# A hybrid Hyena and RG-LRU block: side work handed out at the middle and the end of each in-projection block, gates one lane's gate at a time

## The chip, the core and the metric

One core of a Trainium2 chip. The metric is device time of one execution in us. The engines are TensorE (PE in the profile; its weight loads are PEld), VectorE (DVE), ScalarE (ACT), GpSimd (POOL) and SyncE (SP, which here only issues DMAs). Each engine works through its own queue in order.

## What is computed

One layer of a diffusion block over 4096 latent tokens (width 1024) and 256 context tokens. A modulated RMSNorm feeds one in-projection whose 3072 columns are six groups of 512: `x0`, `x1`, `v` and gate `zh` of a long convolution (done as an FFT), `xr` and gate `zr` of a two-directional gated recurrence. In short:

```
p = (rms_norm(x) * (1 + sc) + sh) @ w_in
xc = dwconv(xr); r = sigmoid(xc @ wa + ba); i = sigmoid(xc @ wx + bx)      # per head, per direction
a = exp(-8 * r * softplus(-lam)); b = sqrt(1 - a*a) * (i * xc); h = scan(a, b)
y = concat(rms_norm(long_conv(v * x1) * x0) * silu(zh), rms_norm(h_fwd + h_bwd) * silu(zr))
out = rms_norm(x + g * (y @ w_out))
```

## The kernel before, in words

Values are split into two f16 halves, so a product is three matmuls (hi*hi, hi*lo, lo*hi). Channels lie on the 128 partitions; a group of 512 columns is four blocks `j` (`NB` = 4), and tokens come in eight chunks `i` of 512 (`NB` and `i` make one **in-projection block**: `inproj`, 8 x 3 = 24 matmuls of 128x512 into a PSUM tile `mm`, of which there are three).

**Pass A** (`pass_a`) goes through chunks 0 to 7, 12 blocks each: four of `xr`, then `x1` and `v` alternating. `OX[i]` says how many of the others go ahead of `xr`. After each block come its short convolution (`conv`, ScalarE then VectorE) and stores. Beside the blocks run: the load, normalisation and split of the next chunk's input tile X (`xload` at places `XK`, its squares on ScalarE, L429, at a later step, then `xsplit` with GpSimd's `xlo` and transposing DMAs into X); the forward recurrence of the chunk (`units_a`, two `unit`s of two lanes each); the Hyena filter (`filter_group`: four exponentials into `dec` on ScalarE every `FD` = 4.95 steps; `filter_row`: three matmuls into `fa`, `kd`, `kh`; its `second` part three matmuls into `fb`, an evacuation `vk`, a store to VkD). The context tokens go once through `ctx_in` in chunk 0.

**Pass B** (`blocks_b`) goes through 24 triples (chunk, name) of four blocks each, `zr`, `x0`, `zh` from chunk 7 down, with the backward recurrence (`units_b`), and pulls FFT steps from a generator: `rate` per block, first 64 steps of `s1u_gen` (two matmuls into `fa`, evacuation `vo`), then slots (`slot_gen`: five loads, 24 small matmuls into `fa` and `fb`, an inverse of a slot before, stores), then parts of the inverse. **Phase out** does the last FFT part and the out-projection; the change does not touch it.

**`unit`** is a generator with one stage per `next`: split of `xc` into `xh`; the gates (per lane and gate three matmuls `xh,gh` into `fa` for the gate written to `R` or `fb` for `I`, and a sigmoid, L824, that empties the bank; then `pmul` on GpSimd); tanh, exp and a square; sqrt; the scan (L849, then `car`, L851). Two units run side by side in a `zip`, so one `next` issues a stage of both.

**The order of the work** is set by a step counter: `at(d, f)` files `f` under the step `d` from now, and `tick`, called after each block, runs what is due. `DA` holds the steps of the recurrence after the last `xr` block in chunk 0, chunk 1 and the others, `DC` those of the context, `DS` and `D0` those of pass B. Side matmuls go through `mms`, which files them 64 instructions later in priority than they stand; a planner then orders each engine's queue when the program is built, by priority and by what its own model says is ready. PSUM has eight banks: three `mm`, two `fa`, two `fb` and one `sm`.

Of the kernel before, what the change touches and what calls it, by code (L numbers as in the profile page):

```python
# [42 lines left out]
FL = (2, 3)  # L43
SIDE = 64
FG = 2
OX = (0, 0, 0, 0, 0, 0, 2, 0)
ET = mybir.EngineType
MS = ()
XS = ((1, 2), (1, 2))
# [1 line left out]
FD = 4.95  # L51
XK = ((6, 9), (1, 6))
NX = 11
D0 = (8, 11, 12, 13, 14, 16, 17, 17)
WO = (9, 13, 16)
SEQ = [(2, "zr"), (2, "x0"), (1, "x0"), (1, "zr"), (0, "x0"), (0, "zh"), (0, "zr"), (2, "zh"), (1, "zh")]
XL = [(6, "zr"), (5, "zr"), (4, "zr"), (3, "zr"), (2, "zr"), (1, "x0"), (0, "x0"), (2, "zh")]
DS = (1, 4, 7, 7, 9, 9, 10)
DA = ((11, 12, 14, 15, 15), (3, 4, 4, 6, 6), (0, 3, 5, 6, 8))
EPS = 1e-6  # L60
MAGIC = 1.5 * 2.0 ** 23
INV2PI = 1.0 / (2.0 * math.pi)
# [100 lines left out]
class K:  # L163
# [334 lines left out]
            w[5] = self.tap_scales(pool, name, j, es[:, 0:1], be[:, 0:1])  # L498
        yield w

    def inproj(self, w, xs):
        ps = self.pst("mm", 3)
        c = 0
        for x in xs:
            n = x.shape[-1]
            i = 0
            for k in range(8):
                for (wi, xi) in ((0, 0), (0, 1), (1, 0)):
                    self.mm(ps[:, c:c + n], w[0][:, wi, k, :], x[:, xi, k, :], i == 0, i == 23)
                    i += 1  # L510
            c += n
        return ps
# [48 lines left out]
    def at(self, d, f):  # L561

        self.todo.setdefault(self.step + d, []).append(f)

    def tick(self):
        for f in self.todo.pop(self.step, []):
            f()
        self.step += 1
# [10 lines left out]
    def pass_a(self):  # L579
        tc, nc, a = self.tc, self.nc, self.a  # L580
        with ExitStack() as es, ExitStack() as right:
# [79 lines left out]
            for i in range(8):  # L661
                xcs = []
                for k, nm in enumerate(names[4:4 + OX[i]] + names[:4] + names[4 + OX[i]:]):
                    if i < 7 and k in XK[i > 0]:
                        h = XK[i > 0].index(k)
                        if h == 0:
                            Xn = self.xtile()
                        xr = self.xload(ap, tok(4 * (i + 1) + 2 * h), 4 * (i + 1) + 2 * h, lag=XS[i > 0][0])
                        self.at(XS[i > 0][1], lambda xr=xr, d=dst(Xn, 2 * h): self.xsplit(ap, xr, self.s1, self.sx, d, IA[1]))
                        if h and i < 5:  # L670
                            self.at(XS[i > 0][1] + 1, lambda i=i, X=Xn: nc.sync.dma_start(self.XD[i + 1], X))
                    j = nm[1]
                    ps = self.inproj(W[nm], [X])
                    p0 = 512 * i - 1 + (1 if i == 0 else 0)
                    if nm[0] == "xr":
                        if j % 2 == 0:
                            xcs.append(hy.tile([128, 1028], F32, name="xc", bufs=4))
                        t = xcs[-1]
                        n = 511 + (i > 0) + (i == 7)
                        c0 = n * (j % 2)  # L680
                        halo[nm] = self.conv(hy, f"xr{j}", ps, W[nm][5], 3, i, i == 7, halo[nm], t, c0 - (i == 0))
                        nc.sync.dma_start(self.xcD[j][:, p0:p0 + n], t[:, c0:c0 + n])
                        if j == 3:
                            for t, d in enumerate(DA[min(i, 2)]):
                                if t == 0:
                                    us = []
                                    self.at(d, lambda us=us, p0=p0, n=n, xcs=xcs: us.append(self.units_a(self.rn, p0, n, xcs)))
                                self.at(d, lambda us=us: next(us[0]))
                    else:
                        b = {"x1": 4, "v": 8}[nm[0]]  # L690
                        t = hy.tile([128, 514], F32, name="cv" + nm[0], bufs=2)
                        halo[nm] = self.conv(hy, f"{nm[0]}{j}", ps, W[nm][5], 2, i, i == 7, halo[nm], t, 0)
                        cnt = 512 - (i == 0) + (i == 7)
                        o = t[:, int(i == 0):int(i == 0) + cnt]
                        if b == 4:
                            o1 = o
                        else:
                            nc.vector.tensor_mul(o1, o1, o)
                            nc.sync.dma_start(self.uD[j][:, p0:p0 + cnt], o1)
                            nc.scalar.activation(o, o1, AF.Square, accum_out=self.usq[:, j, i:i + 1])  # L700
                    if i == 7:
                        self.prep(self.WB, nb[k])
                    self.tick()
                if i >= 6:
                    self.X[i] = X
                X = Xn
# [96 lines left out]

    def unit(self, pool, lanes, n, xc, fin, sig=None):

        nc = self.nc
        L = len(lanes)
        x2 = xc[:, :2 * n]
# [7 lines left out]
        for l, (d, j) in enumerate(lanes):  # L816
            for g, dst, bias in ((0, R, 68 + 4 * d + j), (1, I, 76 + 4 * d + j)):
                for q0 in range(0, n, 512):
                    m = min(512, n - q0)
                    c = n * (j % 2) + q0  # L820
                    ps = self.pst("fa" if g == 0 else "fb", 2)
                    for k, (gi, xi) in enumerate(((0, 0), (0, 1), (1, 0))):
                        self.mms(ps[:, :m], self.gh[d][:, gi, j, g, :], xh[:, 1026 * xi + c:1026 * xi + c + m], k == 0, k == 2)
                    nc.scalar.activation(dst[:, n * l + q0:n * l + q0 + m], ps[:, :m], AF.Sigmoid,  # L824
                                         bias=self.ccol(bias), scale=self.rg[d])
        if sig:
            sig()
        for l in range(0, L, 2):
# [123 lines left out]
    def filter_group(self, pool, g):  # L952

        nc = self.nc
        grp = [4 * g + 4 + k for k in range(4)] if g < 15 else [1, 2, 3, 0]
        hb = self.hb[g % 2]
        n0 = min(grp)
        for h in range(2):
            nc.sync.dma_start(hb[64 * h:64 * h + 64, :, :, 64 * h:64 * h + 64],
                              self.hD[64 * h:64 * h + 64, :, n0:n0 + 4, :])  # L960
        dec = pool.tile([128, 4, 512], F32, name="dec", bufs=1)
        for k, n in enumerate(grp):
            nc.scalar.activation(dec[:, k], self.dl, AF.Exp, scale=self.dcol[:, n:n + 1])
        for k, n in enumerate(grp):
            self.at(1 + k, lambda k=k, n=n: self.filter_row(pool, n, hb[:, :, n - n0, :], dec[:, k]))

    def filter_row(self, pool, n, hb, dec):
        nc = self.nc
        if len(self.sec) > 1:
            self.sec.pop(0)()  # L970
        ps = self.pst("fa", 2)
        for x, (hi, wi) in enumerate(((0, 0), (0, 1), (1, 0))):
            self.mms(ps, hb[:, hi, :], self.whl[:, wi, :], x == 0, x == 2)
# [50 lines left out]
    def blocks_b(self, hy, rn):  # L1024
# [9 lines left out]
        for q, (i, nm) in enumerate(seq):  # L1034
# [14 lines left out]
                    self.at(d, lambda g=st[i]: next(g))  # L1049
            for j in range(NB):  # L1050
                w = W[nm, j]
                ps = self.inproj(w, [X[i]])
                if nm == "zr":
                    if j % 2 == 0:
                        z = rn.tile([128, 1024], F32, name="zr", bufs=2)
# [10 lines left out]
                    if i in (5, 4):  # L1066
                        self.pull(gate, 1)
                self.tick()
                done += rate
                while done >= 1:  # L1070
                    done -= 1
                    self.pull(fft, 1)
# [19 lines left out]
    def units_b(self, rn, i):  # L1092
# [14 lines left out]
        def sig(p):  # L1107
            def f():
# [4 lines left out]
        us = zip(*[self.unit(rn, [(1, 2 * p), (1, 2 * p + 1)], 512, xcs[p],  # L1113
                             lambda h, p=p: self.padd(hfs[p], hfs[p], h[:, :1024]), sig(p) if i else None)
                   for p in range(2)])
        for _ in range(4):
            next(us)
            yield
        next(us)
# [431 lines left out]
```

## Time and profile before

| what | value |
|---|---|
| median of 3 runs | 2286.21 us (2283.73 to 2293.96) |
| the profiled execution | 2286.44 us |
| its span, first to last instruction | 2284.6 us |
| mean granted TensorE clock | 0.927 of 2.4 GHz |
| busy: PE, DVE, ACT, POOL | 84%, 66%, 50%, 38% |

The page and the views of the trace are read in this form: an arrow `out<-in` names tiles; a wait "PE fa L168 <- ACT R L824: total, times, longest" is idle time of PE before an instruction that works on `fa`, ended by the ScalarE instruction of line 824 that writes or reads `R`. L168 is the helper through which all matmuls go, so they are told apart by tiles. Times in timelines and windows are us from the start of the span. Windows name busy time in the order PE, PEld, DVE, ACT, POOL. A matmul's own length is longer than its share of TensorE, since matmuls overlap. Pass A's chunk 3 begins at 421.3, chunk 4 at 521.7, chunk 5 at 618.7 and chunk 6 at 723.6.

### The profile page before, as it was taken

To read this page: it belongs to the slowest core of one execution; us is meant where nothing else is said; L and a number is where in the kernel's file an instruction comes from. 1 tells how busy PE (TensorE), PEld (TensorE's weight loads), DVE (VectorE), ACT (ScalarE), POOL (GpSimd) and SP (SyncE) were. 2 spreads that over 40 slices of the span, in tenths; PEclk is the share of its full clock that TensorE was granted. 3 is DMA by queue.
4 is the path that set the end of the run, shared out by engine and by line. 5 is a ranking of instruction groups with operands and counts; after the bars stand their busy time and mean duration, and the time that the engine had idled before them with its cause. 6 is when DMAs were issued, how large, how long until landed. Compare 5 with 4: busy or idle time off the path is not lost. (4 is left out here: it accounts for less than half of the span.)

```text
span 2284.6 us, 30912 instructions
## 1 busy us (share of the span) xinstructions
PE 1920.0 (84%) x10858; PEld 919.7 (40%) x10858; DVE 1498.6 (66%) x2871; ACT 1151.6 (50%) x1803; POOL 862.5 (38%) x571
## 2 busy tenths in 40 slices
PE   6967769989797889878888999797897766999987
PEld 2434324334343334433334555454544433444433
DVE  4895876857576677664644664755756645777776
ACT  3655766665646577575563633645444412422222
POOL 3024655554656453131322443534433321333330
PEclk9988979989898999999899999998998887999999
DMA  9546244435453322566646999899997799454531
GB/s 291 172 115 168 77 137 137 154 81 162 138 150 96 112 87 96 179 196 207 208 143 210 205 217 249 200 227 244 221 257 206 189 270 230 136 163 155 168 120 74
DMA packets 397608, 391.13 MB, mean 171 GB/s; under 512 B 209513, under 2 KB 295935, under 8 KB 392846
## 3 DMA queue, kind: packets, MB, share of 16 engines
q1 hardware_dynamic: 376988, 342.25, 54.2%
q10 hardware_dynamic: 20466, 46.93, 7.2%
q8 instruction: 85, 1.39, 0.3%
q14 instruction: 69, 0.57, 0.1%
HBM read 213.96 MB, written 132.13 MB: 151 GB/s over the span
## 5 line engine op out<-in xcount | busy, mean ns | idle before, releaser
L168 PE MATMUL mm<-X,wh 128*128 128x512 f16 x3072 | 745.8, 389 | 35.4 <-DMA X<-xh 7.5
L168 PEld LDWEIGHTS <-wh 128*128 128x128 f16 x3648 | 326.5, 100 | 466.9 <-issue 102.3
L168 PE MATMUL mm<-X,wz 128*128 128x512 f16 x1536 | 384.8, 395 | 7.5 <-ACT zh L1064 4.5
L168 PEld LDWEIGHTS <-wz 128*128 128x128 f16 x1728 | 159.9, 101 | 226.7 <-issue 58.0
L168 PEld LDWEIGHTS <-hl 128*128 128x128 f16 x1536 | 151.8, 101 | 212.2 <-issue 20.8
L168 PE MATMUL mm<-wz,hl 128*128 128x512 f16 x768 | 181.8, 395 | 18.9 <-DVE hl L1465 13.4
L168 PE MATMUL mm<-X,hl 128*128 128x512 f16 x768 | 179.9, 389 | 7.7 <-DVE wh L1479 5.3
L985 POOL TENSOR_TENSOR kh<-kd,kh 128x512 f16<-128x512 f32 x64 | 84.5, 1321 | 157.4 <-ACT kh L984 157.4
L460 POOL TENSOR_TENSOR I<-I,xc 128x1024 f32<-128x1024 f32 (+3 forms) x36 | 84.1, 2340 | 128.8 <-ACT I L824 114.8
L1241 POOL TENSOR_TENSOR A<-A,B 128x256 f32<-128x256 f32 x64 | 51.0, 797 | 205.9 <-DVE B L1240 187.8
L452 POOL TENSOR_TENSOR xlo<-xt,xh 128x1024 f16<-128x1024 f32 x32 | 76.8, 2414 | 135.8 <-ACT xh L450 135.8
L168 PE MATMUL fb<-tb,vki 128*128 128x128 f16 x768 | 98.1, 225 | 20.6 <-DMA tb<-in_t_s 19.7
L168 PE MATMUL fa<-xh,gh 128*128 128x512 f16 (+3 forms) x228 | 67.4, 396 | 52.2 <-ACT R L824 42.8
L460 POOL TENSOR_TENSOR zr<-zr,sg 128x1024 f32<-128x1024 f32 x16 | 39.1, 2443 | 176.1 <-ACT sg L1110 176.1
L460 POOL TENSOR_TENSOR xh<-R 128x1024 f32<-128x1024 f32 (+2 forms) x34 | 69.4, 2044 | 79.2 <-ACT R L835 77.7
L1252 DVE SCALAR_TENSOR_TENSOR yy<-A,yy 128x512 f16<-128x512 f32 x64 | 57.7, 902 | 62.1 <-ACT yy L1251 62.0
L841 DVE SCALAR_TENSOR_TENSOR xc<-xh,xc 128x1024 f32<-128x1024 f32 (+2 forms) x34 | 58.2, 1714 | 60.7 <-POOL xh L460 60.3
L168 PE MATMUL fa<-tb,vu 128*128 128x128 f16 x768 | 97.0, 225 | 0.0
L457 POOL TENSOR_TENSOR acc<-acc,dec 128x512 f32<-128x512 f32 x64 | 93.7, 1464 | 4.9 <-ACT dec L978 4.9
L849 DVE TENSOR_TENSOR_SCAN I<-R,car,I 128x512 f32<-128x512 f32 (+2 forms) x64 | 94.6, 1502 | 0.1
L168 PEld LDWEIGHTS <-gh 128*128 128x128 f16 x456 | 46.7, 105 | 111.6 <-issue 70.5
L168 PEld LDWEIGHTS <-vki 128*128 128x128 f16 x768 | 76.7, 100 | 33.7 <-issue 24.5
(377 smaller groups left out, 3723.4 us busy)
## 6 DMA issues: line engine op xcount, KB each, us to landing
VkD<-vk SPq DMA_DIRECT2D x64, 256.0 KB, 2.0
VuD<-vo SPq DMA_DIRECT2D x64, 256.0 KB, 2.5
X<-XD SPq DMA_DIRECT2D x8, 2048.0 KB
vu<-VuD SPq DMA_DIRECT2D x128, 128.0 KB, 3.3
vki<-VkD SPq DMA_DIRECT2D x128, 128.0 KB, 3.6
ZD<-zo SPq DMA_DIRECT2D x64, 256.0 KB, 4.3
xt<-in_x SPq DMA_DIRECT2D x30, 512.0 KB, 5.1
XD<-X SPq DMA_DIRECT2D x6, 2048.0 KB
```

Source lines behind the costliest of these rows:

```text
L168: self.nc.tensor.matmul(out, lhsT, rhs, start=start, stop=stop)
L452: nc.gpsimd.tensor_sub(xl, xt, xh)
L457: self.nc.gpsimd.tensor_add(out, x, y)
L460: self.nc.gpsimd.tensor_mul(out, x, y)
L841: nc.vector.scalar_tensor_tensor(Z, M, 1.0, Z, op0=OP.add, op1=OP.mult)
L849: nc.vector.tensor_tensor_scan(f(h), f(r), f(h), 0.0 if c is None else c, op0=OP.mult, op1=OP.add)
L985: nc.gpsimd.tensor_sub(kh[:, 1], kd, kh[:, 0])
L1241: nc.gpsimd.tensor_sub(A[:, :, 0, :], A[:, :, 0, :], B[:, :, 1, :])
L1252: nc.vector.scalar_tensor_tensor(yy[:, :, 1, :], yv, 0.125, yy[:, :, 0, :], op0=OP.mult, op1=OP.subtract)
```

## The change

Each in-projection block gets a second place for side work, ahead of the fifth of its eight k steps: `inproj` calls `mid` there, which runs what `at` has filed under a half step (and `tick` runs it if no block did). In `unit` the gate stage is split: a `yield` after each lane's gate but the last, so 4 stages take the place of 1 for two lanes, 8 for the context's four. The tables `DC`, `DA`, `DS` and `D0` are longer to match and name half steps. In chunk 1 four other blocks go ahead of `xr`. A filter row's `second` goes to the middle of the block whose end runs the next row. In pass B the FFT generator is pulled at both places, with half the rate each.

```
--- before.py
+++ after.py
@@ -26,7 +26,7 @@
 FFT = 1.75
 INV = 1.65
 LAG = 3
-DC = (1, 2, 4, 5, 5)
+DC = (1, 2, 2, 2.5, 2.5, 3, 3, 3.5, 3.5, 4, 5, 5)
 CT = 5
 ML = 1
 MK = 1
@@ -43,7 +43,7 @@
 FL = (2, 3)
 SIDE = 64
 FG = 2
-OX = (0, 0, 0, 0, 0, 0, 2, 0)
+OX = (0, 4, 0, 0, 0, 0, 2, 0)
 ET = mybir.EngineType
 MS = ()
 XS = ((1, 2), (1, 2))
@@ -51,12 +51,12 @@
 FD = 4.95
 XK = ((6, 9), (1, 6))
 NX = 11
-D0 = (8, 11, 12, 13, 14, 16, 17, 17)
+D0 = (8, 11, 11.5, 12, 12.5, 13, 13, 14, 16, 17, 17)
 WO = (9, 13, 16)
 SEQ = [(2, "zr"), (2, "x0"), (1, "x0"), (1, "zr"), (0, "x0"), (0, "zh"), (0, "zr"), (2, "zh"), (1, "zh")]
 XL = [(6, "zr"), (5, "zr"), (4, "zr"), (3, "zr"), (2, "zr"), (1, "x0"), (0, "x0"), (2, "zh")]
-DS = (1, 4, 7, 7, 9, 9, 10)
-DA = ((11, 12, 14, 15, 15), (3, 4, 4, 6, 6), (0, 3, 5, 6, 8))
+DS = (1, 3, 3.5, 4.5, 5.5, 7, 7, 9, 9, 10)
+DA = ((11, 12, 12.5, 13, 13.5, 14, 15, 15), (1, 2, 2.5, 3, 3.5, 4, 5, 6), (0, 2, 2.5, 3.5, 4.5, 6, 7, 9))
 EPS = 1e-6
 MAGIC = 1.5 * 2.0 ** 23
 INV2PI = 1.0 / (2.0 * math.pi)
@@ -498,13 +498,15 @@
             w[5] = self.tap_scales(pool, name, j, es[:, 0:1], be[:, 0:1])
         yield w
 
-    def inproj(self, w, xs):
+    def inproj(self, w, xs, mid=None):
         ps = self.pst("mm", 3)
         c = 0
         for x in xs:
             n = x.shape[-1]
             i = 0
             for k in range(8):
+                if mid and k == 4:
+                    mid()
                 for (wi, xi) in ((0, 0), (0, 1), (1, 0)):
                     self.mm(ps[:, c:c + n], w[0][:, wi, k, :], x[:, xi, k, :], i == 0, i == 23)
                     i += 1
@@ -562,7 +564,12 @@
 
         self.todo.setdefault(self.step + d, []).append(f)
 
+    def mid(self):
+        for f in self.todo.pop(self.step - 0.5, []):
+            f()
+
     def tick(self):
+        self.mid()
         for f in self.todo.pop(self.step, []):
             f()
         self.step += 1
@@ -670,7 +677,7 @@
                         if h and i < 5:
                             self.at(XS[i > 0][1] + 1, lambda i=i, X=Xn: nc.sync.dma_start(self.XD[i + 1], X))
                     j = nm[1]
-                    ps = self.inproj(W[nm], [X])
+                    ps = self.inproj(W[nm], [X], self.mid)
                     p0 = 512 * i - 1 + (1 if i == 0 else 0)
                     if nm[0] == "xr":
                         if j % 2 == 0:
@@ -803,6 +810,7 @@
 
     def unit(self, pool, lanes, n, xc, fin, sig=None):
 
+
         nc = self.nc
         L = len(lanes)
         x2 = xc[:, :2 * n]
@@ -823,6 +831,8 @@
                         self.mms(ps[:, :m], self.gh[d][:, gi, j, g, :], xh[:, 1026 * xi + c:1026 * xi + c + m], k == 0, k == 2)
                     nc.scalar.activation(dst[:, n * l + q0:n * l + q0 + m], ps[:, :m], AF.Sigmoid,
                                          bias=self.ccol(bias), scale=self.rg[d])
+                if (l, g) != (L - 1, 1):
+                    yield
         if sig:
             sig()
         for l in range(0, L, 2):
@@ -962,12 +972,11 @@
         for k, n in enumerate(grp):
             nc.scalar.activation(dec[:, k], self.dl, AF.Exp, scale=self.dcol[:, n:n + 1])
         for k, n in enumerate(grp):
+            self.at(0.5 + k, lambda: len(self.sec) > 1 and self.sec.pop(0)())
             self.at(1 + k, lambda k=k, n=n: self.filter_row(pool, n, hb[:, :, n - n0, :], dec[:, k]))
 
     def filter_row(self, pool, n, hb, dec):
         nc = self.nc
-        if len(self.sec) > 1:
-            self.sec.pop(0)()
         ps = self.pst("fa", 2)
         for x, (hi, wi) in enumerate(((0, 0), (0, 1), (1, 0))):
             self.mms(ps, hb[:, hi, :], self.whl[:, wi, :], x == 0, x == 2)
@@ -1049,7 +1058,15 @@
                     self.at(d, lambda g=st[i]: next(g))
             for j in range(NB):
                 w = W[nm, j]
-                ps = self.inproj(w, [X[i]])
+
+                def mid():
+                    nonlocal done
+                    self.mid()
+                    done += rate / 2
+                    while done >= 1:
+                        done -= 1
+                        self.pull(fft, 1)
+                ps = self.inproj(w, [X[i]], mid)
                 if nm == "zr":
                     if j % 2 == 0:
                         z = rn.tile([128, 1024], F32, name="zr", bufs=2)
@@ -1066,7 +1083,7 @@
                     if i in (5, 4):
                         self.pull(gate, 1)
                 self.tick()
-                done += rate
+                done += rate / 2
                 while done >= 1:
                     done -= 1
                     self.pull(fft, 1)
@@ -1113,7 +1130,7 @@
         us = zip(*[self.unit(rn, [(1, 2 * p), (1, 2 * p + 1)], 512, xcs[p],
                              lambda h, p=p: self.padd(hfs[p], hfs[p], h[:, :1024]), sig(p) if i else None)
                    for p in range(2)])
-        for _ in range(4):
+        for _ in range(7):
             next(us)
             yield
         next(us)
```

## Rows read from the trace of the kernel before

**Rows 1.** The page, its parts 1 (busy time of each engine) and 2 (40 slices)
```profile
PE 1920.0 (84%) x10858; PEld 919.7 (40%) x10858; DVE 1498.6 (66%) x2871; ACT 1151.6 (50%) x1803; POOL 862.5 (38%) x571
...
PEclk9988979989898999999899999998998887999999
```
**Rows 2.** Windows view: stretch and length, engines' busy time (instructions), clock, DMA share, GB/s
```profile
206.00:917.00 711.00, 604.83 (x2803) 264.24 (x2804) 494.09 (x865) 459.07 (x771) 376.18 (x235) 0.92 0.41 121
917.00:1854.00 937.00, 795.35 (x5112) 408.36 (x5110) 551.69 (x867) 471.24 (x683) 315.08 (x221) 0.94 0.81 212
```
**Rows 3.** Waits view of PE from 206 to 917: total, times, longest
```profile
PE fa L168 <- ACT R L824: 32.7, 6, 14.5
PE fb L168 <- DVE car L851: 14.0, 1, 14.0
...
PE fb L168 <- DVE vk L996: 11.0, 2, 10.4
PE mm L168 <- DMA X<-xh: 7.5, 2, 4.9
PE mm L168 <- DMA X<-xlo: 6.5, 4, 2.8
```
**Rows 4.** Windows view of stretches of pass A, five of them with gates
```profile
421.30:473.90 52.60, 51.88 (x228) 22.58 (x229) 47.93 (x77) 27.25 (x51) 28.02 (x20) 0.95 0.53 171
473.90:501.00 27.10, 15.80 (x61) 6.44 (x60) 5.59 (x13) 17.87 (x30) 12.87 (x9) 0.75 0.36 104
501.00:521.70 20.70, 18.32 (x86) 8.16 (x84) 19.96 (x26) 15.52 (x23) 18.20 (x10) 1.00 0.27 63
...
575.80:600.70 24.90, 17.20 (x62) 6.73 (x61) 6.79 (x15) 16.58 (x29) 15.38 (x11) 0.73 0.41 129
...
674.00:702.80 28.80, 14.33 (x56) 5.85 (x55) 5.31 (x11) 16.36 (x29) 14.27 (x11) 0.70 0.40 105
...
780.90:816.50 35.60, 28.30 (x116) 11.94 (x115) 18.87 (x37) 22.30 (x38) 22.36 (x16) 0.90 0.38 106
816.50:821.60 5.10, 5.10 (x25) 2.30 (x24) 1.63 (x3) 5.09 (x9) 1.62 (x1) 1.00 0.40 76
270.70:306.00 35.30, 21.22 (x85) 8.70 (x84) 23.63 (x32) 26.70 (x42) 16.49 (x11) 0.76 0.22 74
```
**Rows 5.** Timeline of PE from 477 to 492: start, length in us, what
```profile
478.02 0.38 PE L168 MATMUL mm<-X,wz 128*128 128x512 f16 x1
489.71 0.59 PE L168 MATMUL fa<-xh,gh 128*128 128x512 f16 x1 [11.30 <-ACT R L824]
```
**Rows 6.** Timeline of ACT from 477 to 492
```profile
484.92 0.60 ACTq L414 DMA_DIRECT2D rp<-in_t_pos  x1
485.57 0.30 ACT L536 ACTIVATE hax<-cvx,sg 128x2 f32<-128x2 f32 x1 [5.21 <-POOL xt L457]
...
487.58 1.28 ACT L824 ACT_TABLE_LOAD   x1
488.88 0.78 ACT L824 ACTIVATE R<-fa,col,p2r_g 128x512 f32<-128x512 f32 x1
```
**Rows 7.** Waits view of PE from 180 to 207 (context gates)
```profile
PE fa L168 <- ACT R L824: 7.2, 2, 6.3
```
**Rows 8.** Windows and waits (PE) of pass B
```profile
1245.00:1700.00 455.00, 402.54 (x2938) 226.90 (x2937) 279.24 (x442) 217.90 (x351) 180.81 (x163) 0.97 0.94 224
...
PE fa L168 <- DVE vo L1201: 32.3, 13, 8.9
PE fb L168 <- DMA tb<-in_t_s: 19.7, 13, 3.4
...
PE fa L168 <- ACT R L824: 3.3, 2, 2.1
```
**Rows 9.** Groups by form, ACT, 206 to 917: table loads
```profile
L963 ACT ACT_TABLE_LOAD x10 | 12.8, 1283 | 0.2
L824 ACT ACT_TABLE_LOAD x8 | 10.3, 1283 | 1.8 <-DVE I L849 1.6
```

More of the change, by code (lines that the diff above doesn't have):

```diff
@@ L28 @@
 LAG = 3
-DC = (1, 2, 4, 5, 5)
+DC = (1, 2, 2, 2.5, 2.5, 3, 3, 3.5, 3.5, 4, 5, 5)
 CT = 5
@@ L45 @@
 FG = 2
-OX = (0, 0, 0, 0, 0, 0, 2, 0)
+OX = (0, 4, 0, 0, 0, 0, 2, 0)
 ET = mybir.EngineType
@@ L53 @@
 NX = 11
-D0 = (8, 11, 12, 13, 14, 16, 17, 17)
+D0 = (8, 11, 11.5, 12, 12.5, 13, 13, 14, 16, 17, 17)
 WO = (9, 13, 16)
@@ L57 @@
 XL = [(6, "zr"), (5, "zr"), (4, "zr"), (3, "zr"), (2, "zr"), (1, "x0"), (0, "x0"), (2, "zh")]
-DS = (1, 4, 7, 7, 9, 9, 10)
-DA = ((11, 12, 14, 15, 15), (3, 4, 4, 6, 6), (0, 3, 5, 6, 8))
+DS = (1, 3, 3.5, 4.5, 5.5, 7, 7, 9, 9, 10)
+DA = ((11, 12, 12.5, 13, 13.5, 14, 15, 15), (1, 2, 2.5, 3, 3.5, 4, 5, 6), (0, 2, 2.5, 3.5, 4.5, 6, 7, 9))
 EPS = 1e-6
@@ L499, in wprep, with inproj @@
         yield w
-    def inproj(self, w, xs):
+    def inproj(self, w, xs, mid=None):
         ps = self.pst("mm", 3)
@@ L507, in inproj @@
             for k in range(8):
+                if mid and k == 4:
+                    mid()
                 for (wi, xi) in ((0, 0), (0, 1), (1, 0)):
@@ L563, in at, with mid @@
         self.todo.setdefault(self.step + d, []).append(f)
+    def mid(self):
+        for f in self.todo.pop(self.step - 0.5, []):
+            f()
     def tick(self):
+        self.mid()
         for f in self.todo.pop(self.step, []):
@@ L672, in pass_a @@
                     j = nm[1]
-                    ps = self.inproj(W[nm], [X])
+                    ps = self.inproj(W[nm], [X], self.mid)
                     p0 = 512 * i - 1 + (1 if i == 0 else 0)
@@ L825, in unit @@
                                          bias=self.ccol(bias), scale=self.rg[d])
+                if (l, g) != (L - 1, 1):
+                    yield
         if sig:
@@ L964, in filter_group @@
         for k, n in enumerate(grp):
+            self.at(0.5 + k, lambda: len(self.sec) > 1 and self.sec.pop(0)())
             self.at(1 + k, lambda k=k, n=n: self.filter_row(pool, n, hb[:, :, n - n0, :], dec[:, k]))
@@ L968, in filter_row @@
         nc = self.nc
-        if len(self.sec) > 1:
-            self.sec.pop(0)()
         ps = self.pst("fa", 2)
@@ L1051, in blocks_b, with mid @@
                 w = W[nm, j]
-                ps = self.inproj(w, [X[i]])
+                def mid():
+                    nonlocal done
+                    self.mid()
+                    done += rate / 2
+                    while done >= 1:
+                        done -= 1
+                        self.pull(fft, 1)
+                ps = self.inproj(w, [X[i]], mid)
                 if nm == "zr":
@@ L1068, in blocks_b @@
                 self.tick()
-                done += rate
+                done += rate / 2
                 while done >= 1:
@@ L1115, in units_b @@
                    for p in range(2)])
-        for _ in range(4):
+        for _ in range(7):
             next(us)
```

## The prediction

> **What bounds the kernel now.** I begin with the page. TensorE's row is busy for 1920.0 of 2284.6 us, 84% [rows 1], so no engine is full and the question is what TensorE waits for. The line PEclk under it shows tenths of the full clock (2.4 GHz); an 8 or a 7 is a slice of 57 us of which part ran at the lower level, 1.2 GHz. Next I cut the span into stages with the windows view. Pass A (chunks 1 to 7) takes 711.00 us with TensorE busy for 604.83; pass B takes 937.00 with 795.35 [rows 2].
>
> Then I ask the waits view for TensorE alone in pass A. First comes tile `fa` waiting for ScalarE's sigmoid that writes `R` (L824): 32.7 us in 6 waits, the longest 14.5; second is `fb` behind VectorE's `car` (L851), one wait of 14.0 [rows 3]. Both are the recurrence gates: `fa` and `fb` are the two PSUM pairs into which the gate matmuls of `unit` write, and the sigmoid is what empties them.
>
> The windows view of chunk 3 shows where this lies. The stretch before its gates (421.3 to 473.9) has TensorE busy for 51.88 of 52.60 us; the stretch with the gates is 27.10 us long, TensorE is busy for 15.80 of it and its mean granted clock is 0.75; afterwards it is busy for 18.32 of 20.70 at 1.00 [rows 4]. So a chunk runs well except where the gates are.
>
> The timelines say why. TensorE's last matmul before the gap starts at 478.02, the next, a gate matmul into `fa`, at 489.71 after 11.30 us, nearly all of the 27.10-15.80=11.3 us idle in that stretch [rows 5]. ScalarE meanwhile stands still, at 484.92 it issues a DMA for `rp`, after an idle time of 5.21 us that the row of its next activation puts down to GpSimd's `xt` (L457); then come a halo, an evacuation, a square for the next X, a table load of 1.28 at 487.58, and at 488.88 the first sigmoid of 0.78 [rows 6]. All eight gate outputs of a chunk (two units, two lanes, two gates) are asked for at one tick, but `fa` and `fb` have two banks each. TensorE fills all four, stands at the fifth group in order, and the main block's matmuls queue behind it. ScalarE is late because the input tiles of the next chunk arrive in the same blocks.
>
> **The change part by part.** *Nothing is removed.* The 24 gate matmuls and eight sigmoids of a chunk are the same. What moves is when they are handed to the planner.
>
> *Gates one at a time, pass A.* In chunks 2 to 7 the gates went out at tick 3 after the last xr block; now at 2, 2.5, 3.5 and 4.5, each time one gate of one lane for both units: two groups, in two banks of one kind. A burst of eight outputs into four banks becomes four of two outputs. The gates of tick 3 ran about a block and a half after it. Shifted alike, the first two places of chunk 3 come before 478 and are through when ScalarE gets late; the last two fall into its late stretch, but each asks for two banks that were last asked for a block or more before. So TensorE can go on with main blocks, which have three banks of their own. What it costs now: idle time is length minus busy in the five stretches [rows 4]: 27.10-15.80=11.3, 24.90-17.20=7.7, 28.80-14.33=14.5, 35.60-28.30=7.3 and 35.30-21.22=14.1, sum 54.9. The rest is the lower clock: 24 weight loads, one per matmul, pass in 5.10 us at clock 1.00 [rows 4], 0.2125 each; 61 matmuls need 13.0 us and took 15.8, so 2.8; the other stretches (62, 56, 116 and 85 matmuls) give 4.0, 2.4, 3.7 and 3.2. Sum 16.1. Together 71 us, the upper bound of this part. The lower bound is below nothing: filter rows use `fa` too, and where a sigmoid is late at the third place the next filter row waits for its bank, and the main block's matmuls wait behind the row. Of four places two are free of the late stretch and two half covered; I take 60%, 42.5 us.
>
> *Order of chunk 1 (`OX`).* Its xr blocks move from places 0-3 to 4-7, so its gates begin some three blocks after chunk 0's scan was issued instead of one. That aims at the 14.0 us wait for `car` [rows 3], already inside the 71. Its own four stores of `xc` move on SP's queue with it and nobody waits for them before pass B: nothing.
>
> *Context gates.* Sixteen outputs asked for in one tick become four places of four; the two waits of `fa` there cost 7.2 us [rows 7]. I take half, 4 us; bounds 0 and 7.2.
>
> *Filter seconds at the middle.* One group of three matmuls, a copy, a subtraction and a store (SP) per row move half a block earlier, in front of the row. Same work, same queue; it separates one use of `fb` from one use of `fa`. I take nothing; the cover is VectorE's and ScalarE's slack around `vk` (waits of 11.0 in all, [rows 3]), and without it up to one such wait, 10.4 us, comes again.
>
> *Pass B.* The gates go from tick 4 to 3, 3.5, 4.5 and 5.5, with the stage after them at 7 as before. FFT steps are pulled at the middle too, with five loads, a transpose and a store on SP's queue for each slot, issued up to half a block earlier or later. From 1245 to 1700 the DMA engines are busy for 0.94 of the time, and in all of pass B the gates wait for L824 for 3.3 us while the slots wait for `tb` for 19.7 [rows 8]. I take nothing. The s1 part before it waits 32.3 us in 13 waits for `vo` [rows 8]; smoother pulls can take at most those, and a new wait of the size of `car`'s (14.0) is the bound on the other side. I take nothing here either, since these waits stand between ScalarE and VectorE evacuations whose number stays.
>
> *Table switches.* Sigmoids in four places instead of one can lie on both sides of the filter's four exponentials. ScalarE has 8 table loads at L824 and 10 at L963 in pass A, 1283 ns each [rows 9]. A group of exponentials comes every five blocks and the window of the four places is 2.5 blocks, so about half the chunks get one pair more: 8 loads, 10 us of ScalarE. It is busy for 459.07 of 711.00 [rows 2], so I take nothing; if every place had a pair of its own, 3x2x1.283=7.7 us a chunk. The Trainium skill (ScalarE: Activation LUTs, Table sets: the hidden batching unit) speaks against the change: it advises to batch activations by set, and gives some 2.66 us for a switch with its drain. By that figure the 8 loads would be 21 us of ScalarE (an estimate from that page), also off the path; the trace shows 1283 ns and almost no idle time before it.
>
> Sum: the profiled execution took 2286.4 us (span 2284.6; the median of the runs is 2286.2, so the sum stands for it as it is). 2286.4 - 42.5 - 4 = 2240.
>
> **The rivals.** *X comes no earlier.* TensorE reaches the next chunk sooner and finds its input tile X unfinished. For it: TensorE already waits 7.5+6.5 us for the transposes into X in pass A [rows 3]. Against it: the square that the sigmoids sit around in chunk 3 belongs to that very preparation, and VectorE, which splits X, was busy for 5.59 of 27.10 us in the gate stretch and for 19.96 of 20.70 after it [rows 4], so it would start sooner. Then only the chunk 1 stretch (half of its 14.1+3.2) and a trifle of the context remain: 2286-10=2276.
>
> *Slower: ScalarE is late four times.* Each place meets a switch and a sigmoid on an engine whose queue is held by something else. The old wait stays at one place and the other three each cost a table load and a sigmoid, 1.28+0.78=2.06 us [rows 6], 6.2 a chunk, in six chunks 37 us; with half of it behind the free banks, 2286+19=2305. It decides once a place costs over 71/5/4=3.6 us. The sentence of the Trainium skill on batching by set would back this one. Against it: the pair of loads is there in half the chunks only, and two banks stand ready at each place.
>
> *The order hardly moves.* Side matmuls are given a later priority by 64 (`mms`), and the planner orders each engine by what its own model says is ready; it may put the four places together again. Then the burst stays: 2284. Against it: places of 1 and 2.5 blocks' distance are 24 to 60 matmuls apart, of the size of that offset.
>
> **How the numbers follow.** Forecast 0.66 (its own range 2198 to 2272: nearly all of 71+7.2 with some of `vo`, down to a fifth of it), X 0.14, slower 0.16, order 0.04. A measurement of this kernel can tell about 0.5%, 11 us. A part of the X case lies beyond that, so faster 0.68, same 0.16, slower 0.16. The range 2198 to 2297 takes in the forecast, X and order; it leaves out most of the slower case and the far end of the faster one.
>
> **What would show it.** Right: in pass A the waits of `fa` for L824 fall from 32.7 to under 14, `car` is gone from the list, no gap of TensorE there is over 8 us, and pass A is 35 to 50 us shorter, with pass B within 10 us. X: the waits for X grow to over 30 us. Slower: table loads at L824 go from 8 to over 20 with several waits of 2 to 5 us. The forecast is wrong if the gate gaps go and pass A keeps its length, or if pass B moves by more than pass A.

## The result, and the profile after

The changed kernel takes 2311.3 us (median of 4 runs, 2304.12 to 2316.76) against 2284.97 (2281.99 to 2293.96, 4 runs) for the kernel before: a ratio of 1.0112, 95% interval 1.0079 to 1.0145. It is slower by 26 us; the forecast was 46 us faster. The profiled execution took 2304.12 us with a span of 2302.3. Its page, parts 1 and 2, against [rows 1]:

```profile
PE 1926.1 (84%) x10858; PEld 924.8 (40%) x10858; DVE 1493.9 (65%) x2871; ACT 1172.9 (51%) x1816; POOL 854.8 (37%) x571
...
PEclk9988989999998999998898989999898888899999
```

The same work, 17.7 us more of span (this execution is the shortest of the four, 7 us below their median). The windows view says where; pass A begins with the first block of chunk 1, pass B ends where the first block of the out-projection begins:

```profile
207.80:923.90 716.10, 613.14 (x2802) 266.12 (x2803) 482.35 (x866) 474.09 (x782) 369.46 (x236) 0.92 0.41 120
923.90:1876.10 952.20, 798.09 (x5136) 412.84 (x5135) 560.15 (x868) 478.06 (x685) 310.89 (x220) 0.92 0.79 208
```

Against [rows 2] pass A is 5 us longer where 42.5 were to be saved, and pass B, where nothing was to be saved, is 15 us longer. Both signs named as "the forecast is wrong if" are there. In pass B the list of waits of TensorE has a new head:

```profile
PE sm L168 <- DVE p2b_yr L189: 47.6, 6, 11.4
PE fa L168 <- DVE vo L1218: 25.4, 10, 5.0
PE fb L168 <- DMA tb<-in_t_s: 16.1, 13, 3.3
```

The same row of the kernel before:

```profile
PE sm L168 <- DVE p2b_yr L189: 15.2, 4, 8.3
```

`p2b_yr` is a tile of the recurrence's yscale, the last stage but the stores: a tiny matmul, 128x1, adds up its sums of squares over the partitions, and it stands in TensorE's queue among the matmuls of the blocks. The timelines show why it now waits. First the kernel before, chunk 6: last gate group, its sigmoid, first scans, and the tiny matmul, which finds its input ready:

```profile
1076.40 0.59 PE L168 MATMUL fb<-xh,gh 128*128 128x512 f16 x2
...
1080.76 0.77 ACT L824 ACTIVATE I<-fb,col,p2r_g 128x512 f32<-128x512 f32 x1
...
1095.38 2.45 DVE L849 TENSOR_TENSOR_SCAN I<-R,car,I 128x512 f32<-128x512 f32 x2
...
1118.28 0.17 PE L168 MATMUL sm<-p2b_yr,onesb 128*128 128x1 bf16 x1
```

Then the changed kernel, the same chunk:

```profile
1101.04 0.59 PE L168 MATMUL fb<-xh,gh 128*128 128x512 f16 x2
...
1101.92 0.77 ACT L832 ACTIVATE I<-fb,col,p2r_g 128x512 f32<-128x512 f32 x1
...
1118.10 2.45 DVE L859 TENSOR_TENSOR_SCAN I<-R,car,I 128x512 f32<-128x512 f32 x2
...
1137.28 0.16 PE L168 MATMUL sm<-p2b_yr,onesb 128*128 128x1 bf16 x1 [9.77 <-DVE p2b_yr L189]
```

The span up to here is longer by about 13 us (chunk 5's first block starts at 1138.1, before at 1125.2), the last gate is later by 24.6, the scan by 22.7. The tiny matmul's tick is the same. In TensorE's queue the planner has put it only 21 main matmuls later: before, it stood behind the third of the 24 of chunk 6's last block, now behind the last. There it waits 9.77 us, with chunk 5's first block behind it.

Pass A is read best from the groups of TensorE, with the idle time just ahead of each. The kernel before:

```profile
L168 PE MATMUL mm<-X,wh 128*128 128x512 f16 x1344 | 326.0, 390 | 26.5 <-DMA X<-xh 7.5 <-DMA X<-xlo 6.5 <-DVE cvv L530 3.6
L168 PE MATMUL mm<-X,wz 128*128 128x512 f16 x672 | 168.8, 388 | 0.0
L168 PE MATMUL fb<-kh,st 128*128 128x512 f16 x192 | 61.1, 392 | 15.4 <-DVE vk L996 11.0 <-POOL kh L985 4.4
L168 PE MATMUL fa<-whl,hb 128*128 128x512 f16 x192 | 60.1, 387 | 6.6 <-DVE kd L975 3.0 <-ACT whl L948 2.7 <-ACT R L824 0.5
L168 PE MATMUL fa<-xh,gh 128*128 128x512 f16 (+2 forms) x108 | 34.4, 417 | 40.3 <-ACT R L824 32.3 <-DVE kd L975 8.0
L168 PE MATMUL fb<-xh,gh 128*128 128x512 f16 (+2 forms) x108 | 33.1, 401 | 14.0 <-DVE car L851 14.0
```

The changed kernel:

```profile
L168 PE MATMUL mm<-X,wh 128*128 128x512 f16 x1345 | 338.6, 400 | 25.0 <-DVE cvv L532 6.6 <-DVE xc L532 6.5 <-DMA X<-xh 4.9
L168 PE MATMUL mm<-X,wz 128*128 128x512 f16 x672 | 165.7, 389 | 9.3 <-ACT xh L429 5.7 <-DVE xc L532 1.9 <-DVE cvx L527 1.7
L168 PE MATMUL fa<-whl,hb 128*128 128x512 f16 x192 | 60.9, 400 | 14.8 <-ACT R L832 13.5 <-DVE whl L959 1.3
L168 PE MATMUL fb<-kh,st 128*128 128x512 f16 x192 | 58.7, 395 | 35.7 <-POOL kh L994 14.6 <-ACT I L832 11.0 <-ACT kh L993 10.0
L168 PE MATMUL fa<-xh,gh 128*128 128x512 f16 (+2 forms) x108 | 29.2, 379 | 10.4 <-DVE cvv L527 4.7 <-DVE kd L984 2.1 <-DVE car L861 2.1
L168 PE MATMUL fb<-xh,gh 128*128 128x512 f16 (+2 forms) x108 | 28.6, 362 | 1.3 <-DVE cvv L527 1.3
```

`xh,gh` are gates, `whl,hb` a filter row, `kh,st` its second part, `mm` the main blocks. The gates did get free: their idle time fell from 54.3 to 11.7 us, by 42.6. The filter's two groups took 28.5 of that back (22.0 to 50.5), now waiting for the very sigmoids `R` and `I` whose banks they share, and for `kh`; the main blocks took 7.8 (26.5 to 34.3). Over all of pass A idle time went from 105.9 to 103.0 us and busy time from 604.9 to 613.1.

### The profile page after: what moved, and what is told of

It reads as the page before. It is cut to its first block, busy times and chain, and to the rows that moved or that the text cites. A ratio compares the mean times of both kernels' runs of the same rounds, so it can differ in the third digit from the quotient of the medians.

```text
span 2302.3 us, 30931 instructions
## 1 busy us (share of the span) xinstructions
PE 1926.1 (84%) x10858; PEld 924.8 (40%) x10858; DVE 1493.9 (65%) x2871; ACT 1172.9 (51%) x1816; POOL 854.8 (37%) x571
## 5 line engine op out<-in xcount | busy, mean ns | idle before, releaser
L168 PE MATMUL mm<-X,wh 128*128 128x512 f16 x3072 | 761.1, 395 | 32.3 <-DVE cvv L532 6.6
L168 PEld LDWEIGHTS <-wh 128*128 128x128 f16 x3648 | 331.7, 102 | 479.1 <-issue 121.4
L168 PE MATMUL mm<-X,wz 128*128 128x512 f16 x1536 | 377.9, 392 | 11.9 <-ACT xh L429 5.7
L168 PEld LDWEIGHTS <-hl 128*128 128x128 f16 x1536 | 151.2, 100 | 213.9 <-issue 24.6
L452 POOL TENSOR_TENSOR xlo<-xt,xh 128x1024 f16<-128x1024 f32 x32 | 69.5, 2189 | 138.8 <-ACT xh L450 138.4
L168 PE MATMUL fb<-tb,vki 128*128 128x128 f16 x768 | 99.6, 226 | 23.6 <-DMA tb<-in_t_s 16.1
L851 DVE SCALAR_TENSOR_TENSOR xc<-xh,xc 128x1024 f32<-128x1024 f32 (+2 forms) x34 | 50.3, 1480 | 88.3 <-POOL xh L460 88.3
L1269 DVE SCALAR_TENSOR_TENSOR yy<-A,yy 128x512 f16<-128x512 f32 x64 | 64.4, 1007 | 46.3 <-ACT yy L1268 45.2
L1256 DVE TENSOR_TENSOR A<-fa,kf 128x512 f32<-128x512 f32 x64 | 43.9, 686 | 69.1 <-ACT kf L1252 67.9
L168 PE MATMUL fb<-kh,st 128*128 128x512 f16 x192 | 58.7, 395 | 35.7 <-POOL kh L994 14.6
L168 PE MATMUL fa<-xh,gh 128*128 128x512 f16 (+3 forms) x228 | 62.0, 385 | 29.2 <-ACT R L832 8.3
```

What stands on the lines that cost most here:

```text
L168: self.nc.tensor.matmul(out, lhsT, rhs, start=start, stop=stop)
L452: nc.gpsimd.tensor_sub(xl, xt, xh)
L851: nc.vector.scalar_tensor_tensor(Z, M, 1.0, Z, op0=OP.add, op1=OP.mult)
L1256: nc.vector.tensor_mul(A, u4, kf[:, :, 0:1, :].to_broadcast([128, NB, 2, 64]))
L1269: nc.vector.scalar_tensor_tensor(yy[:, :, 1, :], yv, 0.125, yy[:, :, 0, :], op0=OP.mult, op1=OP.subtract)
```

## The experiments

Theories. **M**: pass B makes the loss, its late recurrence being met by TensorE at yscale, and pass A's part neither costs nor gains. **F**: the filter's second parts at the middle cost. **X**: what holds a chunk of pass A is the preparation of the next input tile, so the gate waits only show it. **L**: lateness of pass B's gates costs, not their splitting. Each profiled execution was cut as above; the lengths are in us.

| kernel | ratio to before (95%) | pass A | pass B |
|---|---|---|---|
| before | 1 | 710.8 | 937.3 |
| after | 1.0112 (1.0079 to 1.0145) | 716.1 | 952.2 |
| `a_only` | 0.9999 (0.9984 to 1.0015) | 717.1 | 931.0 |
| `b_only` | 1.0077 (1.0053 to 1.0101) | 709.7 | 953.0 |
| `second_end` | 1.0059 (1.0038 to 1.0079) | 703.0 | 958.3 |
| `b_late` | 1.0107 (1.0081 to 1.0133) | 717.5 | 947.2 |
| `b_gates` | 1.0130 (1.0097 to 1.0163) | 712.4 | 961.8 |
| `b_fft` | 1.0030 (1.0010 to 1.0051) | 710.7 | 942.4 |
| `a_end` | 0.9966 (0.9949 to 0.9984) | 701.2 | 941.9 |
| `bg_early` | 0.9997 (0.9979 to 1.0015) | 712.5 | 937.8 |
| `burst_late` | 1.0121 (1.0096 to 1.0145) | 710.0 | 970.8 |
| `bg_shift` | 1.0053 (1.0033 to 1.0074) | 710.6 | 938.0 |
| `burst_shift` | 1.0024 (1.0009 to 1.0040) | 713.7 | 932.0 |
| `xk_before` | 0.9983 (0.9966 to 1.0000) | 718.3 | 928.7 |
| `xk_a_end` | 1.0014 (0.9992 to 1.0035) | 712.5 | 947.8 |

A caution for the two right columns, which come from one execution each. Where their code is that of the kernel before, pass A began between 205.9 and 212.2 us, pass A took 709.7 to 713.7, pass B 928.7 to 947.8 (`a_only`, `a_end`, `xk_before`, `xk_a_end`) and Phase out 423 to 434. So a length of pass B alone is not read to better than some 10 us either way, and the ratios carry the argument.

**Halves of the change.** `a_only` keeps pass A's and the context's part; `b_only` keeps pass B's. Edits to the changed kernel, `a_only`:

```
-DS = (1, 3, 3.5, 4.5, 5.5, 7, 7, 9, 9, 10)
+DS = (1, 4, 7, 7, 9, 9, 10)
-D0 = (8, 11, 11.5, 12, 12.5, 13, 13, 14, 16, 17, 17)
+D0 = (8, 11, 12, 13, 14, 16, 17, 17)
-                if (l, g) != (L - 1, 1):
+                if split and (l, g) != (L - 1, 1):
...
-                ps = self.inproj(w, [X[i]], mid)
+                ps = self.inproj(w, [X[i]], self.mid)
...
```

`b_only`, the other way round:

```
-DC = (1, 2, 2, 2.5, 2.5, 3, 3, 3.5, 3.5, 4, 5, 5)
+DC = (1, 2, 4, 5, 5)
-OX = (0, 4, 0, 0, 0, 0, 2, 0)
+OX = (0, 0, 0, 0, 0, 0, 2, 0)
-DA = ((11, 12, 12.5, 13, 13.5, 14, 15, 15), (1, 2, 2.5, 3, 3.5, 4, 5, 6), (0, 2, 2.5, 3.5, 4.5, 6, 7, 9))
+DA = ((11, 12, 14, 15, 15), (3, 4, 4, 6, 6), (0, 3, 5, 6, 8))
...
-            self.at(0.5 + k, lambda: len(self.sec) > 1 and self.sec.pop(0)())
...
```

> The change in pass A and the context alone (gates split, DA, DC, OX, filter seconds at the middle); pass B as before. Theory M (the loss of 26 us is made in pass B, where the gates end 1.5 blocks later while the matmul that waits for p2b_yr stays at its tick; pass A merely trades its gate waits for others): 2285 to 2295, pass A within 8 us of the kernel before, p2b_yr waits back at about 15 us. Rival P (spreading costs everywhere, in pass A too): 2300 or more, pass A 10 us or more longer.

> The change in pass B alone (gates split, DS, D0, FFT steps pulled at both places); pass A as before. Theory M: 2298 to 2312, nearly all of the loss, p2b_yr waits of 40 us or more in all. Rival P: about half of it, 2292 to 2300.

Measured: 2283.41 and 2303.05 us beside 2283.98 for the kernel before. All of pass A's new order is worth nothing (M had 2285 to 2295), and pass B's part, within M's range, makes 19 us of the loss (`p2b_yr` waits 42.8 us). Together they lose 26; the intervals of the two ratios overlap, so whether the 7 between are real is not shown. M holds in that the loss is made in pass B.

**The filter's second parts back at the block's end**, the rest as changed (`second_end`):

```
-            self.at(0.5 + k, lambda: len(self.sec) > 1 and self.sec.pop(0)())
...
     def filter_row(self, pool, n, hb, dec):
         nc = self.nc
+        if len(self.sec) > 1:
+            self.sec.pop(0)()
```

> The changed kernel with the filter's second part back at the head of its row, at the end of a block. Theory F (in pass A the gate waits were replaced by waits of the second's matmuls for kh, 15 and 10 us against 4 and 0 before, because they now stand half a block earlier): waits of fb for kh fall from about 25 to under 8 us and pass A gets 10 to 20 us shorter, 2292 to 2302. Rival X (pass A's length is set by the preparation of the next chunk's X, whatever the side work does): pass A within 5 us of the changed kernel, other waits in place of those for kh, 2306 to 2314.

Measured: 2296.01 us, 15 below the changed kernel (12 by the ratios). Its group of second parts in pass A:

```profile
L168 PE MATMUL fb<-kh,st 128*128 128x512 f16 x192 | 61.3, 400 | 23.1 <-ACT I L832 13.3 <-POOL kh L995 9.8
```

Idle 23.1 us against 35.7; the wait for ScalarE's `kh` is gone, that for GpSimd's `kh` stands at 9.8 where F had under 8, and pass A is 13 us shorter. F holds for this part of the loss.

**Yscale alone later**, in the changed kernel (`b_late`):

```
-DS = (1, 3, 3.5, 4.5, 5.5, 7, 7, 9, 9, 10)
+DS = (1, 3, 3.5, 4.5, 5.5, 7, 7, 9, 10.5, 11)
```

> The changed kernel with the last two stages of pass B's recurrence 1.5 and 1 steps later (yscale at 10.5, store at 11 instead of 9 and 10). Theory M: the waits for p2b_yr fall from 47.6 to under 25 us (the last chunk, whose table D0 stays, keeps its 10) and the time falls by 10 to 20 us, 2291 to 2301. Rival S (the halved FFT pulls cost pass B its time, p2b_yr is only where TensorE happens to stand): the waits fall but others take their place, 2306 to 2315.

Measured: 2304.29 us, 1.0107. The waits for `p2b_yr` fell from 47.6 to 21.7 us and the time hardly moved; waits at other places of the same stretch grew (`cva` from 3.3 to 12.8, `zo` from 8.7 to 12.9), and TensorE's idle time in all of pass B fell by 5.2 us only (154.1 to 148.9). The time lies between M's range and the rival's. So M in its narrow form, that the time is lost at this one matmul, falls: it shows the lateness, but freeing it alone does not give the time back.

**Pass B's two parts alone**, on the order of the kernel before: gates split (`b_gates`, new `DS` and `D0`, FFT pulled once a block) and FFT pulled at both places (`b_fft`, old `DS` and `D0`, gates whole). `b_gates` is `b_only` with

```
...
-                ps = self.inproj(w, [X[i]], mid)
+                ps = self.inproj(w, [X[i]], self.mid)
...
-                done += rate / 2
+                done += rate
```

and `b_fft` is `b_only` with

```
-DS = (1, 3, 3.5, 4.5, 5.5, 7, 7, 9, 9, 10)
+DS = (1, 4, 7, 7, 9, 9, 10)
...
```

> Of the change, the split gates of pass B alone (DS, D0, four stages); FFT steps are pulled once per block and pass A is as before. Theory G (the gates end 1.5 blocks later and the matmul of p2b_yr keeps its tick, so TensorE waits in order): 2295 to 2305, most of the 18 us that pass B's part cost, p2b_yr waits of 30 us or more. Rival H (the FFT pulls at two places cost it): 2281 to 2290, and p2b_yr near the 15 us of before.

> Of the change, the FFT pulls at the middle and the end of pass B's blocks alone; gates in one stage with the old tables, pass A as before. Theory G: within 6 us of the kernel before, 2278 to 2290. Rival H: 2295 to 2305, with the loss between block 164 and 176 of the slots.

Measured: 2312.8 and 2292.5 us beside 2283.47. The gates make the loss, more of it than theory G had; the pulls alone cost 0.3%, between the two forecasts. With both, `b_only` loses less (19 us) than the gates alone (29); why is open.

**Pass A's gates split, the filter's second parts at the end, pass B as before** (`a_end`; the edits of `a_only` and `second_end`):

> The change in pass A with the filter's second part at the end of a block as before, pass B as before. Theory F (the seconds' place gave back what the spread gates won): faster than before by 8 to 16 us, 2268 to 2277, pass A near 703 us. Rival (the 10 us that the same edit brought to the whole change were a re-ordering of that one program): 2280 to 2288.

Measured: 2275.82 us, faster than both kernels, by 0.34% of the one before. Pass A is 701.2 us, and what it waits for has moved again:

```profile
PE fa L168 <- DVE kd L985: 15.9, 5, 5.4
PE fb L168 <- ACT I L832: 15.7, 5, 5.2
PE mm L168 <- DVE xc L532: 14.4, 6, 5.5
PE mm L168 <- DMA X<-xh: 10.6, 3, 6.8
...
PE mm L168 <- DMA X<-xlo: 6.2, 5, 2.5
```

**Without the preparation of X** from chunk 2 on, in the kernel before and in `a_end` (`nox_before`, `nox_a_end`):

```
...
+                        if i:
+                            Xn = X
+                        else:
+                            xr = self.xload(ap, tok(4 * (i + 1) + 2 * h), 4 * (i + 1) + 2 * h, lag=XS[i > 0][0])
...
```

> The kernel before, but from chunk 2 on pass A takes the input tile X of chunk 1 again: loads, squares, normalisation, split and transposes of X are left out for six chunks, so the output is another one. Theory X (the preparation of X holds ScalarE and GpSimd and so makes the gate waits): chunks 2 to 6 fall from about 97 to 85 us or less each and the wait of fa for the sigmoid in pass A falls from 33 to under 12 us; pass A shorter by 50 us or more. Rival (the waits come from the burst of eight gate outputs itself): the waits of fa for the sigmoid stay at 20 us or more, pass A shorter by less than 25 us.

> Pass A with the split gates, the filter's second part at the end of a block, pass B as before, and X of chunk 1 used again from chunk 2 on, so that its preparation is left out for six chunks and the output is another one. Theory X (the preparation of X is what pass A waits for, and the burst of gates only shows it): pass A within 8 us of the 625 us that the kernel before takes without it. Rival (the split gates win by themselves, and X only hides that): pass A 610 us or less.

Measured: one run each, 2182.88 and 2210.58 us. The window of pass A and its waits for sigmoids in `nox_before`:

```profile
205.80:830.60 624.80, 584.76 (x2779) 261.09 (x2780) 409.89 (x727) 413.89 (x702) 256.11 (x163) 0.97 0.26 91
...
PE fa L168 <- ACT R L827: 11.0, 4, 6.5
```

Pass A is 86 us shorter, with the burst of gates still there: the waits for `R` fall from 32.7 us [rows 3] to 11.0 with no change to the gates. ScalarE is busy for 45 us less, VectorE for 84 and GpSimd for 120; TensorE is idle for 40.0 us in place of 105.9 and busy for 20 less. With the gates split pass A takes 632.2 us, so splitting wins nothing once the preparation is gone. X holds for pass A. Of the 28 us between the two runs only 7 lie there; 12 lie in pass B and 7 in Phase out, where their code is the same, and with one run of each this stays open.

**Split but not late** (`bg_early`), **late but not split** (`burst_late`), and **both with every later stage moved too** (`bg_shift`, `burst_shift`); pass A, filter and FFT pulls as before, so only `DS` differs, and in step with it `D0`, the last chunk's table:

```
 before       DS = (1, 4, 7, 7, 9, 9, 10)
 bg_early     DS = (1, 2.5, 3, 3.5, 4, 7, 7, 9, 9, 10)
 burst_late   DS = (1, 5.5, 7, 7, 9, 9, 10)
 bg_shift     DS = (1, 3, 3.5, 4.5, 5.5, 8.5, 8.5, 10.5, 10.5, 11.5)
 burst_shift  DS = (1, 5.5, 8.5, 8.5, 10.5, 10.5, 11.5)
```

> Pass B's gates split in four but with the last at tick 4, where the single stage stood (2.5, 3, 3.5, 4; the last chunk's 11, 11, 11.5, 11.5 to end ahead of 12); the rest as before. Theory L (what cost 29 us was that the gates end 1.5 blocks later and all that follows them comes late at a TensorE that works in order): 2280 to 2290, waits for p2b_yr near the 15 us of before. Rival D (the splitting itself costs: sigmoids among other ScalarE work, banks held at four places): 2300 to 2312 again.

> Pass B's gates in one stage as before, but at tick 5.5 instead of 4 (the last chunk's at 13 instead of 12); the rest as before. Theory L: 2303 to 2318, waits for p2b_yr of 30 us or more, with no splitting at all. Rival D: within 8 us of the kernel before.

> Pass B's split gates at the change's places (3 to 5.5) with every later stage of the recurrence 1.5 steps later too (8.5, 8.5, 10.5, 10.5, 11.5; the last chunk's one step later from its tanh on); the rest as before. Theory L in its narrow form (only the wait for p2b_yr counts): near before, 2281 to 2291, p2b_yr under 20 us. Theory L in a wide form (a later recurrence meets the FFT slots and the next chunk at a worse place): p2b_yr falls, yet 2295 to 2308.

> Pass B alone, gates unsplit at 5.5 as in burst_late, and every stage behind them a block and a half later too; pass A as before. Theory L (the loss comes from gates that move while tanh, root, scan and yscale keep their places): pass B is back at 937 us within 6, p2b_yr waits under 15 us, the time within 0.4% of the kernel before (2275 to 2292). Rival (a recurrence that ends a block and a half later costs by itself, wherever its stages stand): pass B 945 to 955, time 2292 to 2302, with the waits at cva, vo or the slots.

Measured, beside 2283.2 to 2283.6: 2282.04, 2313.26, 2295.6 and 2289.65 us. TensorE's waits in pass B, `bg_early`:

```profile
PE sm L168 <- DVE p2b_yr L189: 12.8, 3, 8.7
```

`burst_late`:

```profile
PE sm L168 <- DVE p2b_yr L189: 43.2, 6, 10.5
PE fa L168 <- DVE vo L1211: 26.5, 14, 4.6
PE fb L168 <- DMA tb<-in_t_s: 21.4, 16, 3.6
```

`burst_shift`:

```profile
PE fa L168 <- DVE vo L1211: 40.5, 14, 8.5
PE fb L168 <- DVE zo L1276: 19.3, 9, 4.9
PE mm L168 <- DVE cva L554: 12.2, 4, 4.0
PE fb L168 <- DMA tb<-in_t_s: 8.3, 7, 2.3
...
PE mm L168 <- DVE p2b_yr L189: 6.5, 1, 6.5
```

Split gates that end at tick 4 cost nothing. One unsplit stage at 5.5 costs the whole loss. The same late stage with tanh, root, scan and yscale moved along as well costs 6 us instead of 30, and pass B is back at 932 us. For the split gates the same move brings the loss from 29 us (`b_gates`) to 12 (`bg_shift`). So L holds: most of the loss comes from the distance between the gates and the stages behind them. What is left, 0.24% and 0.53%, is not explained. `bg_shift` lies in the range of L's wide form, by which a later recurrence costs by itself, yet in its profile pass B is back at 938.0 us; 5.9 us more lie ahead of pass A, where TensorE's instructions are those of the kernel before in the same order, and 2.7 in Phase out.

**X loaded at other places** (`xk_before` on the kernel before, `xk_a_end` on `a_end`), same work, one block earlier at the first place of a chunk and two at the second:

```
-XK = ((6, 9), (1, 6))
+XK = ((6, 9), (0, 4))
```

> The kernel before with one tuple changed: the next X is loaded at places 0 and 4 of a chunk instead of 1 and 6. Theory X (the preparation of X, falling on the gates, makes the gate waits): the ScalarE part of it leaves the gate stretch in part, waits of fa for R in pass A fall from 32.7 to under 20, pass A 690 to 703 us, time 2264 to 2276. Rival (the same work only collides with the xr blocks and their convolutions, or the input tile's buffers are not free at place 0): pass A 705 to 718, time 2280 to 2292.

> a_end (gates of pass A one at a time, second part of a filter row at the block's end, pass B as before) with the next X loaded at places 0 and 4. Theory X: the waits of mm for X, 11.5 and 6.2 us in a_end, fall under 8 together, pass A from 701 to 685 to 695, time 2260 to 2270. Rival: X is not what ends late, or it collides elsewhere: pass A 697 to 710, time 2272 to 2285.

Measured: 2278.78 and 2286.84 us beside 2283.6. The groups of gates and of second parts in `xk_before`:

```profile
L168 PE MATMUL fb<-kh,st 128*128 128x512 f16 x192 | 62.0, 391 | 25.5 <-POOL kh L985 15.0 <-ACT kh L984 10.2 <-ACT I L824 0.3
L168 PE MATMUL fb<-xh,gh 128*128 128x512 f16 (+2 forms) x108 | 34.1, 425 | 14.6 <-DVE vk L996 14.6
L168 PE MATMUL fa<-xh,gh 128*128 128x512 f16 (+2 forms) x108 | 33.6, 421 | 30.2 <-ACT R L824 17.2 <-DVE kd L975 12.9
```

The waits for `R` halve (32.7 to 17.2) and those for X nearly go (14.0 to 3.6, in `xk_a_end` from 16.8 to 1.0), as X expected. But pass A is no shorter in either pair (718.3 against 710.8, 712.5 against 701.2), the times that X forecast did not come (`xk_a_end` lies above its rival's too), and `xk_a_end` is slower than `a_end` by 11 us, clear of noise (its profiled execution is the longest of its runs, 9 us above their median). In these two tries the place of the preparation decided which group waits and did not shorten the stage; leaving it out did. Which part of it (squares and copies on ScalarE, scaling on VectorE, sums and the low half on GpSimd, the transposes) sets the length was not tried apart.

## Why the prediction was wrong, step by step

*Gates one at a time, pass A (42.5 us of 71).* **This step failed**, not in what happens at the gates but in what follows. The gate groups lost 42.6 us of idle time. That this is the 42.5 of the forecast is luck: 42.5 was 60% of 54.9 idle and 16.1 of clock, so 33 of idle. What failed is taking idle time in front of the gates as time that the chunk would lose. The lower bound named the mechanism ("filter rows use `fa` too, and where a sigmoid is late at the third place the next filter row waits for its bank") but was not given a size: 28.5 us went to the filter's groups. And what makes ScalarE late, the preparation of the next X, stayed as it was; without it pass A is 86 us shorter (`nox_before`). Chunk 3, the example, shows it: its 11.3 us gap is gone [rows 5], and it takes 100.5 us, as before (52.6+27.1+20.7=100.4, [rows 4]). Its window, and three rows of TensorE's timeline in it:

```profile
424.20:524.70 100.50, 87.36 (x371) 37.42 (x370) 69.70 (x113) 57.88 (x99) 54.49 (x36) 0.92 0.43 133
...
483.63 1.46 PE L168 MATMUL fa<-xh,gh 128*128 128x512 f16 x6
...
487.52 1.46 PE L168 MATMUL fb<-xh,gh 128*128 128x512 f16 x6
...
494.94 1.44 PE L168 MATMUL fb<-kh,st 128*128 128x512 f16 x3 [5.32 <-ACT I L832]
```

The first two places did not come before 478 (chunk 3 itself starts 2.9 us later), and the second is not through when ScalarE gets late: its sigmoids begin at 494.11, after a wait that ScalarE's timeline puts down to `xt` as in [rows 6], and a second part of the filter waits for their bank.

The 16.1 us for the lower clock did not come either: pass A's mean clock stayed at 0.92 and its matmuls are busy for 8.2 us more (the last section says why).

*Order of chunk 1.* The wait for `car` went (`fb<-xh,gh` 14.0 to 1.3) and chunk 1 is 16.6 us shorter (129.1 to 112.5), but chunk 2 is 18.0 longer (85.9 to 103.9): the recurrence of chunk 1 now ends there. Chunk 2 has 28 matmuls more, TensorE is busy in it for 12.5 us more and idle for 5.4 more.

*Context gates (4 us).* The wait of `fa` there is 6.8 us after 7.2 [rows 7]: nothing.

*Filter seconds (nothing; bound 10.4).* Mis-sized. The cover was said to be slack around `vk`; the wait for `vk` did go, but `kh` of the row before is not ready half a block earlier: waits for it rose from 4.4 to 24.6 us, and moving them back is worth 12 to 15 us in the changed kernel and 8 in pass A's part alone (`a_only` to `a_end`).

*Pass B (nothing).* **The second step that failed:** "the stage after them at 7 as before". The last gate moved from 4 to 5.5, and that nothing is late at 7 was argued only from the sigmoids' own waits (3.3 us, [rows 8]), not from the end of the chain, yscale, that TensorE meets in order. The view of waits behind [rows 8] had the row that prices it, `p2b_yr`, 15.2 us; it is not among the rows shown there, nor in the prediction. The bound for a new wait was 14.0; the waits for `p2b_yr` grew by 32.4 and the time by up to 30 (`burst_late`).

*Table switches (8 loads).* There are 30 loads where 18 stood [rows 9]:

```profile
L973 ACT ACT_TABLE_LOAD x16 | 20.5, 1283 | 3.5 <-POOL xt L457 3.3
L832 ACT ACT_TABLE_LOAD x14 | 18.0, 1283 | 8.9 <-POOL xt L457 8.7
```

That is twelve more, 15 us of ScalarE. The Trainium skill (ScalarE: Activation LUTs, Table sets: the hidden batching unit) advises to batch activations by set, since functions of different sets need a load each. The trace agrees in the count: the loads rose with the sigmoids spread among the exponentials. No run takes them away alone; `a_end`, in which ScalarE is busy for 20 us more of pass A than before, is faster all the same.

*The rivals.* The slower rival was right in sign and near in size (2305) but not in mechanism: it put the loss in pass A's sigmoids, with over 20 loads at their line (14). "X comes no earlier" had 10 us of gain where pass A's part alone brought none (2283.41 in `a_only`), and its sign, waits for X of over 30 us, is not there: they fell from 14.0 to 8.0 (`X<-xh` 4.9, `X<-xlo` 3.1), and with the second parts at the end (`a_end`) stand at 16.8. The order did move.

## What to carry to other kernels

Idle time in front of one group is not time saved if its cause is an engine that also serves the next group: sum the idle time over all groups of the stage, before and after, or leave the suspected work out once and see what the stage loses. When a stage of a chain moves in a hand-written order, move every later stage with it (here 6 us of loss in place of 30), or let it end where it ended (here none), and look for the small instruction at the chain's end that stands in a full engine's queue. Price that from its own row of waits before the change.

## What was not expected of the hardware

The 2803 matmuls of pass A were busy for 604.9 us before and for 613.1 after with the same mean granted clock of 0.92, and the mean matmul of `mm<-X,wh` went from 390 to 400 ns. The clock records of the two traces show where the slow time fell. At the lower level (1.2 of 2.4 GHz) pass A spent 114.7 us before and 109.2 after. But before, TensorE was idle in 53.7 us of it, after in 31.1, so it was busy at the lower level for 61.0 us and then for 78.1. At half the clock the 17.1 us between them hold 8.5 us of loss (an estimate from the two levels), which is the 8.2 measured. Of the `mm<-X,wh` matmuls 60 began at the lower level before and 115 after. The gaps at the gates were in good part slow time in which nothing ran; without them the slow time was hardly shorter, and main matmuls ran in it. What sets the length of the slow time was not tried.
